# Light experts on their own TensorE arm, and wider rows of expert weights

## The chip, the cores and the metric

The kernel runs on one core of one Trainium2 chip. The metric is device time in microseconds (us) of one execution. Matrix work runs on PE (its weight loads appear as PEld), elementwise work on DVE and ACT, a little on POOL; SP issues the transfers from HBM.

## The reference, cut to what matters

A trunk of two layers: each has a token mixer and a feed-forward part. That of the first layer is dense; that of the second, which the change touches, is a mixture of eight experts with two experts for each of 256 tokens. Everything is float32.

```
D_MODEL, D_FF, N_EXPERTS, TOP_K, SEQ = 1024, 3584, 8, 2, 256
logits = (hf @ router_w) + router_b
top_logit, top_idx = lax.top_k(logits, TOP_K)
top_w = jax.nn.softmax(top_logit, axis=-1)
# for each expert e, on the tokens that chose it:
y = (jax.nn.silu(xb @ w1[e]) * (xb @ w3[e])) @ w2[e]     # xb: rows x 1024
# each token's output is the sum of its two experts' y, weighted with top_w
```

The three matrices of one expert are 1024x3584, 1024x3584 and 3584x1024 floats, 44.04 MB; those of all eight are read once, 352 MB.

## The kernel before, in words

The program is written in phases. The last, `e1`, is the expert stage: from some 985 us to the end. `route` (line 1158) ranks the experts of each token, computes each token's slot within its expert (`pos`) and the weights. `gather` (line 1246) picks, for two experts at a time, the rows by a matmul with one-hot matrices `pe` (slot number equals `pos`), and leaves them transposed and split in two parts, `gh` and `gl`, since the fast matmul type (fp32r) keeps fewer bits than float32. A product of two float32 matrices is then three fast matmuls: high by high, low by high, high by low.

The weights go through the class `Weights` (line 1198). A unit is 1 MiB, loaded by SP into a ring of buffers named `raw` (11 in this phase), cast to `hi` by ACT in two halves (line 1227, ring `hl` of three), and subtracted to `lo` by DVE in one instruction (line 1231, two buffers). An expert has 42 units: seven blocks of 512 hidden columns, each with two units of w1, two of w3 (four times 128 rows of 512 columns, so rows of 2 KB) and two of w2 (rows of 4 KB). Loads, casts and subtractions are issued in the order of the units; `weights.next` keeps one unit ahead of the one that is multiplied.

For each block `hidden` (line 1315) multiplies w1 (`up`, lines 1291, 1292 and 1294: eight matmuls with the high weights, four with the low ones, for each unit), then w3, and forms silu(a) * b, `s1`, on ACT and DVE. `turned` transposes the block before on PE (line 1331) and splits it (lines 1335, 1336). `down` (lines 1349, 1351) multiplies that by w2 into two PSUM banks that collect over the seven blocks. The matmuls are all 128 rows by 512 columns, whether an expert has 40 rows or 128. `finish` scatters an expert's result back with matmuls (lines 1365, 1366), spread over the next expert by `step`; `finish_last` does so at the end (line 1379). If an expert had over 128 rows, a second pass under `tc.If` (line 1464) would run; its code is jumped over.

What sets the order is the program's text and a scheduler that keeps it on each engine apart from a few priorities; each engine runs its own list and waits on semaphores. A `raw` buffer comes free when DVE has subtracted its unit.

## Time and profile before

| | us |
|---|---|
| median of three runs | 2018.96 (2017.47 to 2019.13) |
| the profiled execution | 2017.74 |
| its span in the trace | 2016.0 |
| expert weights' matmuls in it | 1006.26 to 2000.2 |

| engine | busy us | share of the span |
|---|---|---|
| PE | 1926.9 | 96% |
| DVE | 1601.0 | 79% |
| ACT | 1271.1 | 63% |
| POOL | 49.0 | 2% |

The trace is one execution. Durations of PE overlap, since its matmuls are pipelined, so its pace is read from the starts of neighbouring instructions. "Idle before" is how long an engine stood before an instruction, with the operation that released it. PEclk is the granted TensorE clock as a share of the full one: 1.00 is 2.4 GHz and 0.50 is 1.2 GHz.

### The profile page before, as it was taken

How to read it: one execution, taken by the hardware profiler on the slowest of the kernel's cores; microseconds unless marked ns; L12 is line 12 of the kernel's file. 1: busy time of each engine (PE TensorE's matmuls, PEld its weight loads, DVE VectorE, ACT ScalarE, POOL GpSimd, SP SyncE). 2: the span in 40 equal slices, each digit the busy share in tenths (PEclk: the TensorE clock that was granted, in tenths of full speed). 3: DMA queues.
4: the chain of work that ended last, by engine and by line, in shares of the span. 5: the costliest groups of instructions: out<-in, count | busy, mean ns of one | idle time of the engine just before them, and what ended most of it. 6: DMA issues, size and time to landing. Idle time of an engine off the chain costs nothing.

```text
span 2016.0 us, 36973 instructions
## 1 busy us (share of the span) xinstructions
PE 1926.9 (96%) x15372; PEld 1666.4 (83%) x15372; DVE 1601.0 (79%) x1880; ACT 1271.1 (63%) x1810; POOL 49.0 (2%) x55
## 2 busy tenths in 40 slices
PE   5899999999999899999899999999999999999997
PEld 2889889999998798889778788787887878878785
DVE  3778687787666877787588988889898898898887
ACT  2755655544444755655477777677776777777774
POOL 0101000000000101000000000000000000000000
PEclk8999999999999999999899999999999999999999
DMA  8544546698762544456789999999999999999992
GB/s 279 172 155 129 168 146 221 213 311 272 252 215 86 168 153 137 155 169 219 282 311 373 352 335 358 351 371 347 344 356 346 375 352 329 362 345 381 355 363 83
DMA packets 283540, 538.82 MB, mean 267 GB/s; under 512 B 13602, under 2 KB 120548, under 8 KB 283364
## 3 DMA queue, kind: packets, MB, share of 16 engines
q1 hardware_dynamic: 278448, 536.02, 75.6%
q8 instruction: 122, 2.00, 0.4%
q10 hardware_dynamic: 4916, 0.35, 0.2%
q14 instruction: 54, 0.44, 0.1%
HBM read 535.27 MB, written 1.06 MB: 266 GB/s over the span
## 4 chain that ended last, share of the span: by engine, by line
PE 77%; DVE 12%; ACT 5%; DMA 4%; issue 2%; ACTq 0%; DVEq 0%; POOL 0%; POOLq 0%; SPq 0%
PE g L1294 10%; PE a L1349 10%; PE g L1292 9%; PE g L1291 9%; PE g L375 7%; PE g L379 7%; PE g L377 7%; PE a L1351 5%; DVE lo L1231 3%; DMA raw<-in_moe_w_dram 2%; DVE hl L340 2%; DVE t L627 2%; PE a L1055 1%; PE a L1056 1%; PE a L1057 1%
## 5 line engine op out<-in xcount | busy, mean ns | idle before, releaser
L1231 DVE TENSOR_TENSOR lo<-raw,hl 128x2048 fp32r<-128x2048 f32 (+1 forms) x338 | 755.7, 2274 | 45.5 <-ACT hl L1227 40.5
L1227 ACT CAST hl<-raw 128x1024 fp32r<-128x1024 f32 x672 | 653.6, 1049 | 6.3 <-PE g L1292 4.8
L340 DVE TENSOR_TENSOR hl<-raw,hl 128x1024 fp32r<-128x1024 f32 (+1 forms) x252 | 298.3, 1189 | 135.7 <-ACT hl L339 135.1
L339 ACT CAST hl<-raw 128x1024 fp32r<-128x1024 f32 (+1 forms) x252 | 256.8, 1022 | 199.8 <-PE g L379 132.3
L1292 PE MATMUL g<-hl,r 128*128 128x512 f32 x896 | 349.5, 390 | 1.9 <-DVE r L1282 1.9
L1291 PE MATMUL g<-hl,r 128*128 128x512 f32 x896 | 350.6, 391 | 0.1
L1294 PE MATMUL g<-lo,r 128*128 128x512 f32 x896 | 244.7, 395 | 8.5 <-DVE lo L1231 8.5
L375 PE MATMUL g<-r,hl 128*128 128x256 f32 x1536 | 234.4, 292 | 6.6 <-ACT r L483 3.4
L377 PE MATMUL g<-r,hl 128*128 128x256 f32 x1536 | 227.1, 287 | 0.0
L379 PE MATMUL g<-r,hl 128*128 128x256 f32 x1536 | 222.4, 286 | 0.5 <-DVE hl L340 0.5
L375 PEld LDWEIGHTS g<-r,hl 128*128 128x128 f32 x1536 | 203.4, 193 | 15.4 <-ACT r L483 4.7
L1294 PEld LDWEIGHTS g<-lo,r 128*128 128x128 f32 x896 | 163.9, 188 | 51.0 <-DVE lo L1231 19.8
L377 PEld LDWEIGHTS g<-r,hl 128*128 128x128 f32 x1536 | 203.3, 194 | 2.2 <-issue 1.8
L379 PEld LDWEIGHTS g<-r,hl 128*128 128x128 f32 x1536 | 201.2, 193 | 2.7 <-issue 1.9
L1292 PEld LDWEIGHTS g<-hl,r 128*128 128x128 f32 x896 | 168.2, 188 | 38.1 <-DVE r L1282 2.2
L1291 PEld LDWEIGHTS g<-hl,r 128*128 128x128 f32 x896 | 168.2, 188 | 36.5 <-ACT r L1281 0.4
L1351 PE MATMUL a<-hl,t2r 128*128 128x512 f32 x448 | 174.5, 390 | 0.0
L1349 PE MATMUL a<-hl,t2r 128*128 128x512 f32 x448 | 174.2, 389 | 0.0
L1335 ACT CAST t2r<-a 128x512 fp32r<-128x512 f32 x56 | 32.8, 586 | 161.4 <-PE a L1331 161.4
L1349 PE MATMUL a<-lo,t2r 128*128 128x512 f32 x448 | 125.2, 401 | 2.2 <-DVE lo L1231 2.2
L1351 PEld LDWEIGHTS a<-hl,t2r 128*128 128x128 f32 x448 | 84.0, 188 | 18.0 <-DVE t2r L1336 0.4
L1349 PEld LDWEIGHTS a<-hl,t2r 128*128 128x128 f32 x448 | 84.0, 188 | 17.8 <-ACT t2r L1335 0.2
(321 smaller groups left out, 2122.4 us busy)
## 6 DMA issues: line engine op xcount, KB each, us to landing
raw<-in_moe_w_dram SPq DMA_DIRECT2D x334, 1024.0 KB, 7.5
raw<-in_w_in_dram SPq DMA_DIRECT2D x60, 1024.0 KB, 5.4
raw<-in_ffn_w_dram SPq DMA_DIRECT2D x42, 1024.0 KB, 5.8
raw<-in_ada_w_dram SPq DMA_DIRECT2D x40, 1024.0 KB, 5.6
f<-in_ada_w_dram SPq DMA_DIRECT2D x8, 1024.0 KB, 7.8
raw<-in_w_up_dn_dram SPq DMA_DIRECT2D x8, 1024.0 KB, 4.9
raw<-in_w_out_dram SPq DMA_DIRECT2D x8, 1024.0 KB, 4.8
raw<-in_w_up_sb_dram SPq DMA_DIRECT2D x4, 1024.0 KB, 4.9
```

The costliest lines, as they stand in the source:

```text
L339: A.copy(hv, part)
L340: V.tensor_sub(lv, part, hv.bitcast(F32))
L375: T.matmul(pv[:, b, :], hv[:, k, :], xh[:, k, :], start=(k == 0), stop=False)
L377: T.matmul(pv[:, b, :], hv[:, k, :], xl[:, k, :], start=False, stop=False)
L379: T.matmul(pv[:, b, :], lv[:, k, :], xh[:, k, :], start=False, stop=(k == kc - 1))
L1227: self.hi = A.copy(hi[:, h, :], raw[:, h, :])
L1231: V.tensor_sub(lo[:, h, :], raw[:, h, :], hi[:, h, :].bitcast(F32))
L1291: T.matmul(ps, xh[:, 4 * u + k, :], hv[:, k, :], start=(u == 0 and k == 0), stop=False)
L1292: T.matmul(ps, xl[:, 4 * u + k, :], hv[:, k, :], start=False, stop=False)
L1294: T.matmul(ps, xh[:, 4 * u + k, :], lv[:, k, :], start=False, stop=(u == 1 and k == 3))
L1349: T.matmul(ye[nb], gh[:, gs], w[:, k, nw], start=(f == 0 and u == 0 and p == 0), stop=last)
L1351: T.matmul(ye[nb], gl[:, gs], w[:, k, nw], start=False, stop=False)
```

## The change

Each expert's number of rows is counted in `route`, and a flag for each expert (at most 64 rows) is loaded into eight registers of PE (class `Light`). An expert's work now comes in 21 groups of two units. On PE each group is an If with two arms: `heavy`, the three fp32r matmuls as before, and `few`, which reads the unsplit `raw` weights and unsplit rows (`x32`, `g32`) with plain fp32 matmuls on 64 rows; it puts the two halves of the columns on the two halves of the array, output partitions 0 to 63 and 64 to 127. One matmul with `zero` for each product blanks the part of the banks that `few` leaves unwritten. The slots of light experts are moved (`slots`), so that gathered rows stand twice. ACT and DVE cast and subtract each unit in both cases.

Blocks are 1024 hidden columns now (three, and a last one of 512): w1 and w3 come in rows of 4 KB, w2 with two neighbouring rows per partition, 8 KB. `raw` has 7 buffers instead of 11, `hl` 4 instead of 3, `lo` 4 instead of 2. PSUM banks are four for `g` and four for `a`, instead of two and six. The steps of `finish` and `gather` are called in more places.

```diff
     banks_m = dict(g=2, s=2, a=3, v=1)
     phase_f = dict(raw2=3, hl2=3, r8=2, f4=4, t2=4, t2r=4)
-    phase_b = dict(raw2=8, lo=2, r4=6, t2=5, t2r=6, gt=1, xn=2, pe=2, pte=2)
+    phase_b = dict(raw2=4, hl2=1, lo=4, r4=6, x32=3, s32=1, t2=5, t2r=6, gt=1, xn=2, pe=2, pte=2)

     layout_b = dict(
-        t2r=[P, 512], xn=[P, 2, D], pe=[P, 512], r4=[P, KC, P], t2=[P, 512], pte=[P, S], gt=[P, D], raw2=[P, 2048],
-        lo=[P, 2048],
+        t2r=[P, 512], x32=[P, KC, P // 2], s32=[P, 512], xn=[P, 2, D], pe=[P, 512], r4=[P, KC, P], t2=[P, 512], pte=[P, S], gt=[P, D], raw2=[P, 2048],
+        hl2=[P, 2048], lo=[P, 2048],
...
@@ -1171,7 +1171,12 @@
         ps = bank("a")
         T.matmul(ps[:, 0 : 2 * NE], C["before"], oa.rearrange("p b n -> p (b n)"), start=True, stop=False)
         T.matmul(ps[:, NE : 2 * NE], ones, oa[:, 0, :], start=False, stop=True)
+        pc_ = bank("a")
+        for b in range(2):
+            T.matmul(pc_[:, 0:NE], ones, oa[:, b, :], start=(b == 0), stop=(b == 1))
         V.tensor_copy(pos, ps[:, 0 : 2 * NE].rearrange("p (b n) -> p b n", n=NE))
+        V.tensor_copy(rt[:, 5, 0], pc_[:, 0:NE])
+        light = Light(rt[:, 5, 0])
...
+    class Light:
+
+
+        def __init__(self, cnt):
+            self.flag = pc.tile([P, NE], F32, tag="light", name="light")
+            self.int = pc.tile([P, NE], I32, tag="lighti", name="lighti")
+            V.tensor_scalar(self.flag, cnt, float(P // 2) + 0.5, None, ALU.is_lt)
+            V.tensor_copy(self.int, self.flag)
+            self.back = pc.tile([P, NE], F32, tag="back", name="back")
+            V.tensor_scalar(self.back, self.flag, -float(P // 2), None, ALU.mult)
+            self.regs = [
+                nc.values_load(self.int[0:1, e : e + 1], engines=[mybir.EngineType.PE], min_val=0, max_val=1)
+                for e in range(NE)
+            ]
+
+        def slots(self, e):
+
+            t = mk("t2", [P, 512])[:, 0:P]
+            V.tensor_scalar(t, C["iota"], P // 2 - 0.5, self.back[:, e : e + 1], ALU.is_gt, ALU.mult)
+            V.tensor_add(t, t, C["iota"])
+            return t
+
+        def arms(self, e, light, heavy):
+            with tc.If(self.regs[e] > 0) as cmp:
+                light()
+            with cmp.Else():
+                heavy()
...
         def sources(self, j):
             late = None
             for e in range(NE):
-                for f in range(DFF // 512):
-                    w = slice(512 * f, 512 * f + 512)
+                for f, n in self.blocks:
+                    w = slice(f, f + n)
+                    rows = 2048 // n * P
                     for src in (moe_w1, moe_w3):
-                        for u in range(2):
-                            yield src[j, e][512 * u : 512 * u + 512, w], 4, 512
+                        for u in range(D // rows):
+                            yield src[j, e][rows * u : rows * u + rows, w].rearrange("(k p) n -> p k n", p=P), n
                     if late:
                         yield from late
-                    late = [(moe_w2[j, e][512 * f + 256 * u : 512 * f + 256 * u + 256, :], 2, D) for u in range(2)]
+
+                    late = [
+                        (moe_w2[j, e][f + 256 * u : f + 256 * u + 256, :].rearrange("(p k) n -> p k n", k=2), D)
+                        for u in range(n // 256)
+                    ]
...
+        def unit(self, raw, kc, n, parts):
+
             hi = mk(ring("hl"), [P, kc, n], F32R)
             lo = mk("lo", [P, kc, n], F32R)
             for i in range(2):
                 h = slice(i * kc // 2, (i + 1) * kc // 2)
-                self.hi = A.copy(hi[:, h, :], raw[:, h, :])
+                A.copy(hi[:, h, :], raw[:, h, :])
             with tc.issue_after(self.after.ins) if self.after else nullcontext():
                 for i in range(parts):
                     h = slice(i * kc // parts, (i + 1) * kc // parts)
                     V.tensor_sub(lo[:, h, :], raw[:, h, :], hi[:, h, :].bitcast(F32))
-            return hi, lo
...
+            return raw, hi, lo
+
+        def split(self, n):
+            while len(self.ready) < n and self.loaded:
+                self.ready.append(self.unit(*self.loaded.popleft()))
+
+        def group(self):
+
+            self.load(2)
+            self.split(4)
+            return [self.ready.popleft() for _ in range(2)]
...
+            if e0 == 0:
+                weights.after = last
+            x32 = [mk("x32", [P, KC, HS]) for _ in range(2)]
...
+                    G.tensor_copy(x32[e][:, k2, :], t[:, :, 0:HS])
...
+        def up(e, n):
+
+
+
+
+            xh, xl, x32 = gath[e]
+            banks = [bank("g") for _ in range(n // 512)]
+            kc, half = 2048 // n, n // 2
+
...
+            def heavy(u0, units):
+                for u, (_, hv, lv) in enumerate(units):
+                    for w, xs in ((hv, (xh, xl)), (lv, (xh,))):
+                        for k in range(kc):
+                            kk = kc * (u0 + u) + k
+                            for x_ in xs:
+                                for b, ps in enumerate(banks):
+                                    T.matmul(
+                                        ps, x_[:, kk, :], w[:, k, 512 * b : 512 * b + 512],
+                                        start=(kk == 0 and x_ is xh and w is hv), stop=(kk == KC - 1 and w is lv),
+                                    )
+
...
+            def few(u0, units):
+                wide = len(banks) > 1
+                if u0 == 0 and not wide:
+                    blank()
+                for u, (w, _, _) in enumerate(units):
+                    for k in range(kc):
+                        kk = kc * (u0 + u) + k
+                        for i, h in enumerate(halves):
+                            T.matmul(
+                                banks[0][h, 0:half], x32[:, kk, :], w[:, k, half * i : half * i + half],
+                                start=(wide and kk == 0), stop=(kk == KC - 1), skip_group_check=True,
+                            )
+                if u0 == 0 and wide:
+                    blank()
+
+            for u0 in range(0, KC // kc, 2):
+                units = weights.group()
+                light.arms(e, lambda: few(u0, units), lambda: heavy(u0, units))
+                weights.after = None
+                weights.load(5)
+                yield
+            yield banks

...
+        def turned(banks):
+
+            parts = []
...
+                for c in range(4):
+                    at = c // 2 * 256 + c % 2
+                    T.transpose(pg[:, c * P : (c + 1) * P], s1[:, at : at + 255 : 2], ident)
+                gh = mk("t2r", [P, 512], F32R)
+                gl = mk("t2r", [P, 512], F32R)
+                with tc.high_priority(offset=80):
+                    A.copy(gh, pg)
+                    V.tensor_sub(gl, pg, gh.bitcast(F32))
+                    if j == 0:
+                        g32 = mk("s32", [P, 512])
+                        A.copy(g32, pg)
+                parts.append((gh, gl))
+            return parts, g32
...
+            def few(q, units):
+                if first and q == 0:
                     for nb in range(2):
-                        nw = slice(512 * nb, 512 * nb + 512)
-                        last = f == NF - 1 and u == 1 and p == 3
-                        T.matmul(ye[nb], gh[:, gs], w[:, k, nw], start=(f == 0 and u == 0 and p == 0), stop=last)
-                        if p < 2:
-                            T.matmul(ye[nb], gl[:, gs], w[:, k, nw], start=False, stop=False)
+                        T.matmul(ye[nb], zero, parts[0][0], start=True, stop=True, skip_group_check=True)
+                for u, (w, _, _) in enumerate(units):
+                    i, at = (q, u) if n > 512 else (u, 0)
+                    for k in range(2):
+                        gs = slice((2 * at + k) * P + i * HS, (2 * at + k) * P + i * HS + HS)
+                        for nb, h in enumerate(halves):
+                            T.matmul(
+                                ye[nb][h, :], g32[:, gs], w[:, k, 512 * nb : 512 * nb + 512],
+                                start=False, stop=(last and u == 1 and k == 1), skip_group_check=True,
+                            )
+
+            for q in range(n // 512):
+                units = weights.group()
+                light.arms(e, lambda: few(q, units), lambda: heavy(q, units))
+                weights.load(5)
+                yield
...
+        def hidden(e, n, late):
+
+            p1 = up(e, n)
+            next(p1)
+            g = turned(late[3]) if late else None
+            step()
+            for banks in p1:
+                step()
+            ss = [mk("t2", [P, 512]) for _ in banks]
+            for s1, ps in zip(ss, banks):
+                A.activation(s1, ps, AF.Silu)
+            for banks in up(e, n):
+                step()
+            for s1, ps in zip(ss, banks):
+                V.tensor_mul(s1, s1, ps)
+            return ss, g
...
-    with phase("e1", phase_b, dict(g=2, a=6), layout_b):
+    with phase("e1", phase_b, dict(g=4, a=4), layout_b):
```

On PE, at the start of the first expert, the list of before is below: `up` for the second product of the first block, with `r` the gathered rows' parts, `hl` and `lo` a unit's parts, and `g` the PSUM bank.

```order
L1291 MATMUL g_12351<-hl_12333,r_1366_12198 128x512
L1292 MATMUL g_12351<-hl_12333,r_1367_12199 128x512
L1294 MATMUL g_12351<-lo_12334,r_1366_12198 128x512 x4
L1291 MATMUL g_12351<-hl_12354,r_1366_12198 128x512
L1292 MATMUL g_12351<-hl_12354,r_1367_12199 128x512
L1291 MATMUL g_12351<-hl_12354,r_1366_12198 128x512
```

The list of the changed kernel at the same place, the first group of the first expert: `x` is `x32`, and `raw` the unsplit weights.

```order
L1219 COMPARE_AND_BRANCH
L1372 MATMUL g_12394<-raw_1352_12152,x_1375_12307 64x512 x4
L1372 MATMUL g_12394<-raw_1353_12154,x_1375_12307 64x512 x4
L1359 MATMUL g_12395<-r_1377_12309,zero 128x512
L1219 UNCONDITIONAL_BRANCH
L1351 MATMUL g_12394<-hl_1357_12162,r_1377_12309 128x512
L1351 MATMUL g_12395<-hl_1357_12162,r_1377_12309 128x512
L1351 MATMUL g_12394<-hl_1357_12162,r_1378_12310 128x512
L1351 MATMUL g_12395<-hl_1357_12162,r_1378_12310 128x512
```

Each group is now a compare, a light arm of eight 64-row matmuls (and here the blanking one), a jump, and the heavy arm; the heavy arm alternates between two banks.

On SP, in the middle of the stage, before (a row is one load of 1 MiB; in brackets the semaphores that it waits for):

```order
L324 DMA raw_1511_12962<-in_moe_w_dram 128x2x1024 [waits DMAHW0_49,DVE_49]
L324 DMA raw_1514_12981<-in_moe_w_dram 128x4x512 [waits DMAHW1_49,DVE_49]
L324 DMA raw_1518_13001<-in_moe_w_dram 128x4x512 [waits DMAHW2_49,DVE_49]
L324 DMA raw_1521_13020<-in_moe_w_dram 128x4x512 [waits DMAHW3_49,DVE_49]
L324 DMA raw_1525_13040<-in_moe_w_dram 128x4x512 [waits DMAHW4_49,DVE_49]
L324 DMA raw_1532_13070<-in_moe_w_dram 128x2x1024 [waits DMAHW5_49,DVE_49]
```

And in the changed kernel:

```order
L1219 UNCONDITIONAL_BRANCH
L324 DMA raw_1546_13368<-in_moe_w_dram 128x2x1024 [waits DMAHW2_49,DVE_49,PE_49]
L324 DMA raw_1551_13414<-in_moe_w_dram 128x2x1024 [waits DMAHW3_49,DVE_49,PE_49]
L1219 UNCONDITIONAL_BRANCH
L324 DMA raw_1552_13416<-in_moe_w_dram 128x2x1024 [waits DMAHW4_49,DVE_49,PE_49]
L324 DMA raw_1557_13461<-in_moe_w_dram 128x2x1024 [waits DMAHW5_49,DVE_49,PE_49]
L1219 UNCONDITIONAL_BRANCH
L324 DMA raw_13463<-in_moe_w_dram 128x2x1024 [waits DMAHW6_49,DVE_49,PE_49]
L324 DMA raw_13520<-in_moe_w_dram 128x2x1024 [waits DMAHW7_49,DVE_49,PE_49]
L1219 UNCONDITIONAL_BRANCH
```

A load that waited for an earlier transfer and DVE now also waits for PE, and SP has a jump at each group.

On PE, between routing and gather, in the changed kernel (the list of before goes from line 1173 to the gather at once):

```order
L1142 MATMUL s_11803<-t_1331_12096,rw 8x256 x2
L1152 MATMUL a_12126<-cst,t_1338_12124 128x8 x2
L1172 MATMUL a_12184<-rt,cst 128x16
L1173 MATMUL a_12184<-rt,ones 128x8
L1176 MATMUL a_12187<-rt,ones 128x8 x2
L1207 TENSOR_LOAD lighti
L1207 ISA x2
```

Eight such pairs of a load and two register instructions stand there, ahead of the first matmul of the gather.

## Rows read from the trace of the kernel before

**Rows 1.** The page: busy time; weight loads (count, KB, us to landing)
```profile
PE 1926.9 (96%) x15372; PEld 1666.4 (83%) x15372; DVE 1601.0 (79%) x1880; ACT 1271.1 (63%) x1810; POOL 49.0 (2%) x55
...
raw<-in_moe_w_dram SPq DMA_DIRECT2D x334, 1024.0 KB, 7.5
```

**Rows 2.** By stretch: us, busy of each engine, PEclk, DMA share, GB/s
```profile
1450.00:1700.00 250.00, 247.27 (x1129) 202.62 (x1128) 218.75 (x140) 185.67 (x220) 0.00 (x0) 1.00 0.98 354
1700.00:1950.00 250.00, 247.27 (x1117) 202.15 (x1116) 220.77 (x136) 183.99 (x213) 0.00 (x0) 1.00 0.99 359
```

**Rows 3.** Groups by line, 1450 to 1700 us (count, busy, mean ns, idle before)
```profile
L1231 DVE TENSOR_TENSOR lo<-raw,hl 128x2048 fp32r<-128x2048 f32 x85 | 191.2, 2287 | 10.8 <-ACT hl L1227 10.4 <-DMA raw<-in_moe_w_dram 0.4
L1227 ACT CAST hl<-raw 128x1024 fp32r<-128x1024 f32 x170 | 165.4, 1049 | 1.3 <-PE g L1292 1.3
L1291 PE MATMUL g<-hl,r 128*128 128x512 f32 x225 | 88.0, 391 | 0.0
L1292 PE MATMUL g<-hl,r 128*128 128x512 f32 x225 | 87.7, 390 | 0.0
L1294 PE MATMUL g<-lo,r 128*128 128x512 f32 x226 | 61.9, 395 | 2.0 <-DVE lo L1231 2.0
```

**Rows 4.** Waits of SP, 1450 to 1700 us (us in total, times, longest)
```profile
SPq L324 <- DVE lo L1231: 198.2, 80, 6.9
```

**Rows 5.** Waits of PE, 1014 to 1995 us
```profile
PE g L1294 <- DVE lo L1231: 8.5, 17, 1.1
PE a L1349 <- DVE lo L1231: 2.2, 3, 0.7
```

**Rows 6.** Timeline of PE, 1996 to 2005 us (start, us, line, shapes, count)
```profile
1997.31 0.39 PE L1349 MATMUL a<-hl,t2r 128*128 128x512 f32 x1
...
1998.90 0.39 PE L1351 MATMUL a<-hl,t2r 128*128 128x512 f32 x1
...
2000.81 3.70 PE L1379 MATMUL a<-t,pte 128*128 128x512 f32 x8 [0.62 <-DVE t L1374]
```

**Rows 7.** Timeline of PE, start of the expert stage
```profile
999.66 5.85 PE L1266 MATMUL a<-pe,xn 128*128 128x256 f32 x32 [1.82 <-DVE pe L1251]
...
1006.26 0.51 PE L1291 MATMUL g<-hl,r 128*128 128x512 f32 x1
```

**Rows 8.** Timeline of PE, 24 to 37.5 us: matmuls of the conditioning
```profile
24.14 3.56 PE L252 MATMUL g<-f,r 128*32 128x512 f32 x8 [2.21 <-DMA f<-in_ada_w_dram]
...
33.13 1.91 PE L252 MATMUL s<-f,r 128*32 128x512 f32 x8 [0.67 <-DMA f<-in_ada_w_dram]
```

**Rows 9.** Busy time by stretch, four stretches that differ in PEclk
```profile
24.00:27.50 3.50, 3.36 (x8) 0.55 (x8) 3.40 (x19) 0.00 (x0) 0.00 (x0) 0.50 0.95 301
33.00:37.50 4.50, 3.66 (x16) 0.76 (x16) 0.65 (x1) 0.00 (x0) 0.00 (x0) 1.00 1.05 380
650.00:690.00 40.00, 34.83 (x308) 31.04 (x307) 32.85 (x67) 29.71 (x63) 5.39 (x3) 1.00 0.42 138
985.00:1005.00 20.00, 11.89 (x69) 10.00 (x68) 12.31 (x52) 8.80 (x18) 0.00 (x0) 0.74 0.56 208
```

**Rows 10.** Busy time by stretch, two stretches with a full DMA queue
```profile
966.00:981.00 15.00, 15.00 (x114) 13.14 (x114) 7.67 (x13) 7.91 (x15) 0.00 (x0) 1.00 1.05 390
1449.00:1454.00 5.00, 5.00 (x24) 4.16 (x23) 5.00 (x4) 3.33 (x4) 0.00 (x0) 1.00 1.03 413
```

**Rows 11.** Line 1464, the skip of the second pass (ns, start us)
```profile
L1464 POOLq COMPARE_BRANCH  x1: 45/45/45, 1037.7 to 1037.7; - x1
L1464 PEldq COMPARE_BRANCH  x1: 3345/3345/3345, 2002.1 to 2002.1; - x1
```

**Rows 12.** Instructions of line 1532, behind that skip
```profile
L1532 POOLq DRAIN  x3: 34/41/82, 1037.9 to 2015.7; - x3
```

**Rows 13.** Instructions of line 1463, the register load ahead of it
```profile
L1463 SPq TENSOR_LOAD <-mosti x1: 478/478/478, 1969.5 to 1969.5; - x1
...
L1463 SPq SEQ_ASSERT  x1: 33/33/33, 1970.3 to 1970.3; - x1
```

More of the change, by code (lines that the diff above doesn't have):

```diff
@@ L1184, in route @@
         V.tensor_add(wt, wt, tmp)
-        return oa, wt, pos
-    def fullest(oa):
-        ps = bank("a")
-        T.matmul(ps[:, 0:NE], ones, oa[:, 0, :], start=True, stop=False)
-        T.matmul(ps[:, 0:NE], ones, oa[:, 1, :], start=False, stop=True)
-        most = pc.tile([P, 1], F32, tag="most", name="most")
-        mosti = pc.tile([P, 1], I32, tag="mosti", name="mosti")
-        V.tensor_reduce(most, ps[:, 0:NE], AX.X, ALU.max)
-        V.tensor_copy(mosti, most)
-        return mosti
+        return oa, wt, pos, light
+    zero = pc.tile([P, P], F32R, tag="zero", name="zero")
+    most = pc.tile([P, 1], F32, tag="most", name="most")
+    mosti = pc.tile([P, 1], I32, tag="mosti", name="mosti")
+    class Light:
[20 more added lines that the diff above has]
+                heavy()
     class Weights:
+        blocks = [(1024 * i, min(1024, DFF - 1024 * i)) for i in range(-(-DFF // 1024))]
         def __init__(self, j):
             self.coming = self.sources(j)
-            self.ready = deque()
-            self.hi = self.after = None
+            self.loaded, self.ready = deque(), deque()
+            self.after = None
         def sources(self, j):
@@ L1231, in unit, with experts @@
                     V.tensor_sub(lo[:, h, :], raw[:, h, :], hi[:, h, :].bitcast(F32))
-            return hi, lo
-        def fetch(self, n):
-            while len(self.ready) < n and (src := next(self.coming, None)):
-                self.ready.append(self.unit(*src))
-        def next(self):
-            self.fetch(1 + 1)
-            return self.ready.popleft()
-    def experts(l, weights, xnh, xnl, oa, wt, pos, merge):
-        NF = DFF // 512
+            return raw, hi, lo
[6 more added lines that the diff above has]
+            return [self.ready.popleft() for _ in range(2)]
+    def experts(l, weights, xnh, xnl, oa, wt, pos, light, merge):
+        blocks = weights.blocks
         pes = {}
+        HS = P // 2
+        halves = [slice(0, HS), slice(HS, P)]
         def gather(e0):
@@ L1283, in gather @@
             for e in range(2):
-                gath[e0 + e] = parts[e]
-        def up(xh, xl):
-            ps = bank("g")
-            for u in range(2):
-                hv, lv = weights.next()
-                for k in range(4):
-                    T.matmul(ps, xh[:, 4 * u + k, :], hv[:, k, :], start=(u == 0 and k == 0), stop=False)
-                    T.matmul(ps, xl[:, 4 * u + k, :], hv[:, k, :], start=False, stop=False)
-                for k in range(4):
-                    T.matmul(ps, xh[:, 4 * u + k, :], lv[:, k, :], start=False, stop=(u == 1 and k == 3))
-            return ps
+                gath[e0 + e] = *parts[e], x32[e]
@@ L1423, in moe @@
         weights = Weights(j)
+        G.memset(zero.bitcast(F32), 0.0)
         with tc.high_priority(offset=0):
-            weights.fetch(2)
-        oa, wt, pos = route()
+            weights.load(5)
+            weights.split(2)
+        oa, wt, pos, light = route()
         xnh = mk("xn", [P, 2, D], F32R)
@@ L1465, in moe @@
             V.tensor_scalar(pos, pos, float(-P), None, ALU.add)
-            experts(l, Weights(j), xnh, xnl, oa, wt, pos, merge)
+            V.tensor_scalar(rt[:, 5, 0], rt[:, 5, 0], float(-P), None, ALU.add)
+            weights = Weights(j)
+            weights.load(5)
+            weights.split(2)
+            light = Light(rt[:, 5, 0])
+            experts(l, weights, xnh, xnl, oa, wt, pos, light, merge)
     with phase("m0", phase_m, banks_m):
```

105 lines of the change are left out of this document (54 added, 51 removed).

## The prediction

> **What bounds the kernel now.** The page first: PE is busy 96% of the span, and no other engine comes near [rows 1]. Then the expert stage alone, since the change touches nothing else. In a stretch of 250 us there PE is busy 247, DVE 219, ACT 186, and the DMA queue moves 354 GB/s [rows 2]. The groups of that stretch say what fills the engines [rows 3]: DVE subtracts 85 units of 1 MiB at 2.287 us, ACT casts them in two halves of 1.049 us, and PE runs three matmuls for each chunk and unit. The waits of SP show that the loads stand at the buffers: 198 us of waiting for DVE's subtraction of an older unit [rows 4]. So the DMA share near 1 is a queue that is kept full, not a queue that limits. PE itself waited 8.5 and 2.2 us for a `lo` in the whole stage [rows 5]. PE is the bound there, and DVE follows 12% behind it.
>
> How fast PE goes is read from starts, not from durations, since matmuls overlap: seven steps take 1998.90 − 1997.31 = 1.59 us, 0.227 us for each 128x512 matmul [rows 6]. An expert has 42 units and 504 such matmuls: 114.4 us. The stage's weight matmuls run from 1006.26 to 2000.2 us (2000.81 less the idle 0.62) [rows 6, 7], 994 us for eight experts, so 124.2 for one and 248.5 for two. Of the 124.2, 114.4 are weight matmuls, 1.3 the waits for `lo`, and some 8.5 the transposes, gathers and closings.
>
> **Who takes which arm.** The reference's inputs route 77, 41, 65, 56, 80, 43, 90 and 60 rows to experts 0 to 7 (worked out from the reference). Experts 1, 3, 5 and 7 have at most 64: four light experts, in turn with four heavy ones. No expert has over 128, so the second pass is still skipped.
>
> **A light expert on PE.** The three matmuls of 0.227 us per 512 columns and chunk go, and an fp32 matmul on 64 rows comes, for two column halves at once. The trace of before has no 64-row pair, so two rows bound it. A whole-width fp32 matmul shows as two records, one after the other: 8 records in 3.70 us, 0.44 us each [rows 6]. The conditioning matmuls are fp32 too, with 32 output rows in neighbouring column groups: there 8 records take 1.91 us though each lasts 0.59, so (1.91 − 0.59)/3 = 0.44 for each two records, two at a time [rows 8]; the clock was at full there [rows 9]. The change has 84 such couples for each expert. With overlap a couple is 0.88 us: 84 × 0.88 = 73.9 us, and the blanking matmuls (2.3 by ten of 0.227) and the 8.5 of other work bring it to 85. Without overlap it is 168 × 0.88 + 11 = 159. I take 85, since the row nearest in kind (fp32, partial columns, neighbours) shows the overlap; 159 is a rival below.
>
> **What is late next in a light expert.** Not PE. The splits stay: ACT and DVE still split each unit, read or not. DVE needs 219 us for each 250 of the stage [rows 2], so 218 for a pair and 109 for one expert, plus two slot operations of at most 0.7 us; ACT needs 42 × 2 × 1.049 = 88 and four more casts of 0.6. The loads are 44.04 MB for one expert: at 390 GB/s (2 KB rows, queue full) 113 us, at 413 (w2's 4 KB rows) 107, and at the stage's mean of 354, 124 [rows 2, 10]. The rows now come as 4 and 8 KB, so I take 400, about the middle of the two full stretches: 110. DVE and DMA thus both ask for about 110, and a light expert costs 111. Buffers can shift this: PE enters a light expert with up to four split units and more landed ones ahead of it, and may leave it ahead of DVE, since the light arm waits for the load alone. That is at best 105, or less with the debt paid at the start of the next heavy expert; a pair cannot fall below DVE's 218 to 222 or the load's 88.08 MB / 0.400 = 220. I keep 111, since once a block PE's transposes wait for DVE's product of the two hidden banks, and DVE has splits of later groups ahead of it: that keeps PE from leaving DVE far behind.
>
> By the Trainium skill (DMA: Bandwidth & Descriptors, Specifications) HBM gives one core about 358 GB/s; by that a light expert would be 123 us and the whole some 2010. The stretches of 390 and 413 GB/s [rows 10] disagree with it as a limit for this core, and the measurement decides; the rule's result stands below as the weak case.
>
> **A heavy expert.** The same 504 matmuls, in blocks of 1024 columns, with `hl` and `lo` four deep instead of three and two: 114.4 + 8.5 = 123, the `lo` waits gone. New are 21 group boundaries, each a compare and a jump on PE. Branches of before: POOL's jump over about 12 instructions of the built program started at 1037.7 and its next instruction stood at 1037.9; PE's over about 4,500 took 3.345 us [rows 11, 12]. A group's arm is at most some 24 matmuls, so the near row is nearer: 0.2 us, two for a group, 0.4 × 21 = 8 us if bare. I cost them at nothing, because PE's sequencer runs ahead of its array: its branch of 2002.1 was issued while the matmuls of line 1379 ran until 2000.81 + 3.70 = 2004.51, a lead of 2.4 us [rows 6, 11]. Cover gone, 123 becomes 127 to 131. The other engines get 168 jumps each too; on DVE, the second bound, 21 × 0.2 = 4 us for an expert if nothing covers them.
>
> **Buffers and the added wait.** `raw` goes from 11 units to 7, and a load now waits for PE as well as for DVE; behind it on SP stand all later loads, and for those PE and both splitters wait. In a heavy expert up to four of the seven can lie split but unpassed, which leaves three on their way: three units in a landing time of 7.5 us [rows 1] are 420 GB/s, over the 358 that 44.04 MB in 123 us asks for. So I cost it at nothing in a heavy expert; if it binds, loads fall back to the stage's 354, which is the weak case. The gather's POOL copies and the extra `s32` cast run on engines with room [rows 1, 3].
>
> **The start.** PE gets eight register loads between the routing's matmuls and the gather. SP's like load took 0.478 us, and its check stood 0.8 us behind the load's start [rows 13]: 8 × 0.85 = 7 us, and the 1.8 us that PE waits ahead of the gather anyway [rows 7] can cover some. Between 0 and 8, I take +6.
>
> **The sum.** A pair is 123 + 111 = 234 instead of 248.5: −14.5, four times −58. The last expert is light and nothing heavy comes behind it, so its lead of some three units need not be paid back: −8. The start +6. Together −60 against the profiled execution: 2017.74 − 60 = 1957.7. The median stands 1.2 above that execution, so 1959, **1960** rounded.
>
> **The rivals.**
> (a) *Branches are dear.* If a group's two jumps cost as PE's far one, 2 × 3.345 − 2.4 = 4.3 us in each of 84 heavy groups: +361, about 2320, and more with DVE's and ACT's jumps in the light ones. It decides from 0.7 us per heavy group (84 × 0.7 = 59 eats the gain). For it: all long branches of this trace are dear [rows 11]. Against: POOL's near one is not [rows 12]. The Trainium skill (Runtime: NRT & Kernel Launch, Instruction fetch mechanics) says that a taken branch stalls when its target lies outside the window of instructions on hand; POOL's and PE's rows agree with it, and by it most jumps over one arm would be free, those that leave the window not. A middle case, one in five of the 168 jumps of heavy groups dear: 34 × 3.3 = 112 bare, or 34 × 0.9 = 31 behind the lead, so 1990 to 2070.
> (b) *The column halves do not overlap.* Light PE 159: a pair is 123 + 159 = 282, +34, with the start 2017.74 + 134 + 6 = 2158. Against: [rows 8].
> (c) *The clock falls in light experts.* PE would work 85 of 111 us, in bursts of 3.5 us (74 in 21 groups) with about 1.2 us idle between. At low clock the same conditioning matmuls took 3.56 us against 1.91 [rows 8, 9], (3.56 − 1.06)/3 = 0.83 for two records; a light expert would be 84 × 1.66 + 20 = 160, all in all 2160. It decides when more than half of the light work runs low. For it: a stretch in which PE was busy 11.89 of 20 us showed a mean clock of 0.74. Against: one with 34.83 of 40 kept 1.00 [rows 9]; 85 of 111 lies between, nearer to the second.
> (d) *Weak.* Loads keep to 354 to 360, or some branches are bare: light 118 to 124, heavy 123 to 127, 1990 to 2014.
> (e) *No change*: what the light arms give, boundaries take.
>
> **How the numbers follow.** Forecast (1925 to 1990, the low end from pairs at 222 with the last expert's lead) 0.66; weak 0.11; no change 0.04; slower 0.19, of which branches 0.08, clock 0.06, no overlap 0.05. The range **1925 to 2030** leaves out the far parts of the slower cases. A measurement of this kernel tells about 0.2% from no change, so faster 0.77 (forecast and weak), same 0.04, slower 0.19.
>
> **What would show it.** In a heavy expert: starts 0.227 us apart, no idle time of PE at the 21 boundaries, about 123 us from first to last weight matmul. In a light one: two records every 0.44 us, granted clock 1.00, about 111 us, the queue at 390 GB/s or more, PE idle on loads or SP on DVE. The gather at most 8 us later. I am wrong if boundaries show idle time of over 0.7 us (a), if light records come one at a time (b), if the clock row falls in every second eighth of the stage (c), or if light experts stand near 124 us with the queue near 355 GB/s (d).

## The result

| | before | after |
|---|---|---|
| median of the runs, us | 2019.05 (four) | 1971.37 (four, 1966.01 to 1972.13) |
| profiled execution: time, span, us | 2017.74, 2016.0 | 1972.13, 1970.3 |
| mean granted clock of the span | 0.986 | 0.965 |

The changed kernel takes 0.9752 of the time of before, 95% interval 0.9723 to 0.978: 47.7 us less, where 59 were forecast, and inside the range of 1925 to 2030.

The page of the changed kernel answers to [rows 1]: PE is still the busiest engine, but no longer by much, and a unit of weights lands in 7.0 us, before in 7.5.

```profile
PE 1823.6 (93%) x14868; PEld 1412.8 (72%) x14868; DVE 1599.0 (81%) x1900; ACT 1283.3 (65%) x1842; POOL 80.0 (4%) x88
...
raw<-in_moe_w_dram SPq DMA_DIRECT2D x334, 1024.0 KB, 7.0
```

The stretches below are cut at the first weight matmul of an expert: a heavy expert, a light one, and the last light one (columns as in [rows 2]).

```profile
1244.50:1364.80 120.30, 119.87 (x540) 96.07 (x538) 107.73 (x66) 92.24 (x107) 0.00 (x0) 1.00 0.98 369
1364.80:1483.50 118.70, 101.90 (x461) 42.09 (x460) 110.76 (x82) 96.35 (x121) 10.17 (x8) 0.91 0.97 371
1842.70:1950.60 107.90, 92.60 (x423) 36.32 (x422) 106.83 (x66) 91.39 (x106) 0.00 (x0) 0.95 0.97 385
```

In the heavy stretch PE is busy 119.9 of 120.3 us, as it was in the whole stage before. In the light one it is busy 101.9 of 118.7, at a mean clock of 0.91, and DVE, with 110.8, is the busiest engine. The queue moves 371 GB/s there, against 354 in [rows 2]. This pair takes 239.0 us, and the other middle pair, from 1483.52 to 1722.42, takes 238.9; before they took 249.9 and 249.4. (Cut in this way, one group of the heavy expert's second product lies in the light stretch, and one of the light expert's in the next heavy one, so these two numbers mix the arms by some 2 us; their sum does not.)

The beginning and the end of the stage, from PE's timeline:

```profile
998.34 0.61 PE L1172 MATMUL a<-rt,cst 128*128 128x16 f32 x2 [3.65 <-DVE rt L1170]
...
999.22 1.00 PE L1176 MATMUL a<-rt,ones 128*128 128x8 f32 x4
1006.72 5.76 PE L1314 MATMUL a<-pe,xn 128*128 128x256 f32 x32 [6.51 <-issue]
...
1012.86 2.08 PE L1351 MATMUL g<-hl,r 128*128 128x512 f32 x8
```

```profile
1943.74 3.65 PE L1454 MATMUL a<-raw,s 128*64 128x512 f32 x16
1950.64 3.65 PE L1454 MATMUL a<-raw,s 128*64 128x512 f32 x16 [3.25 <-ACT s L1420]
1955.13 3.70 PE L1493 MATMUL a<-t,pte 128*128 128x512 f32 x8 [0.84 <-DVE t L1488]
```

The gather starts 7.1 us later than in [rows 7], behind 6.5 us without a matmul, and the first weight matmul stands at 1012.86 instead of 1006.26. The weights end at 1955.13 − 0.84 = 1954.3 instead of 2000.2. So the start costs 6.6, the stage falls from 993.9 to 941.4 us, and the tail behind it is as long as before. Of the 6.6 us, 1.5 lie ahead of the register loads: the matmuls of line 1172 start at 998.34, and in the trace of before at 996.82.

The light arm's own rows are the couples. Sixteen records take 3.65 us (the row at 1943.74), two at a time: (3.65 − 0.59) / 7 = 0.44 us for each two, which is what the conditioning matmuls showed in [rows 8].

The register loads and the branches of PE (the times in ns are shortest, median, longest):

```profile
L1207 PEldq TENSOR_LOAD <-lighti x8: 297/302/492, 1000.9 to 1005.9; - x8
```

```profile
L1219 PEldq COMPARE_BRANCH  x252: 65/179/413, 1010.9 to 1950.7; - x126
```

The eight register loads start 0.71 us apart (1000.9 to 1005.9). The 252 compares and jumps on PE took at most 0.41 us and 0.18 in the median, where the far one of [rows 11] took 3.3.

The longest waits that answer to [rows 4, 5], over the whole stage (total us, times, longest):

```profile
PE a L1412 <- DVE t L1519: 34.5, 12, 5.0
```

```profile
SPq L324 <- PE g L1351: 268.5, 109, 12.5
SPq L324 <- DVE lo L1271: 231.9, 156, 3.3
SPq L324 <- PE a L1443: 120.2, 28, 5.1
```

PE now waits above all at line 1412, the transposes, for DVE's product of the hidden banks (line 1519). Loads wait for PE more than for DVE.

### The profile page after: what moved, and what is told of

Same layout as the page of the kernel before. It is cut to its first block, busy times and chain, and to the rows that moved or that the text cites. A ratio compares the mean times of both kernels' runs of the same rounds, so it can differ in the third digit from the quotient of the medians.

```text
span 1970.3 us, 36475 instructions
## 1 busy us (share of the span) xinstructions
PE 1823.6 (93%) x14868; PEld 1412.8 (72%) x14868; DVE 1599.0 (81%) x1900; ACT 1283.3 (65%) x1842; POOL 80.0 (4%) x88
## 4 chain that ended last, share of the span: by engine, by line
PE 63%; DVE 18%; ACT 8%; issue 7%; DMA 4%; DVEq 0%; SPq 0%; ACTq 0%
PE g L1351 15%; PE g L379 7%; PE g L375 7%; PE g L377 7%; DVE lo L1271 7%; PE a L1438 4%; PE g L1372 3%; ACT hl L1267 3%; DMA raw<-in_moe_w_dram 2%; PE a L1454 2%; PE a L1443 2%; DVE t L627 2%; DVE hl L340 2%; ACT hl L339 1%; PE a L1055 1%
## 5 line engine op out<-in xcount | busy, mean ns | idle before, releaser
L1351 PE MATMUL g<-hl,r 128*128 128x512 f32 x896 | 222.9, 391 | 0.0
L1372 PE MATMUL g<-raw,x 128*64 128x512 f32 (+1 forms) x1024 | 212.1, 563 | 0.0
L1351 PEld LDWEIGHTS g<-hl,r 128*128 128x128 f32 x896 | 167.4, 188 | 37.0 <-ACT hl L1267 2.4
L1372 PEld LDWEIGHTS g<-raw,x 128*64 128x64 f32 x1024 | 71.5, 141 | 114.6 <-issue 104.2
L1454 PE MATMUL a<-raw,s 128*64 128x512 f32 x448 | 120.2, 684 | 3.6 <-ACT s L1420 3.2
L1351 PE MATMUL g<-lo,r 128*128 128x512 f32 x448 | 120.7, 391 | 0.5
L1351 PEld LDWEIGHTS g<-lo,r 128*128 128x128 f32 x448 | 83.6, 188 | 20.0 <-DVE lo L1271 2.9
L210 DVE SCALAR_TENSOR_TENSOR f<-raw,csil,f 128x1024 f32<-128x1024 f32 x70 | 92.5, 1322 | 5.7 <-DMA raw<-in_ada_w_dram 5.2
L1438 PE MATMUL a<-hl,t2r 128*128 128x512 f32 x224 | 89.0, 397 | 1.7 <-ACT hl L1267 1.7
L1454 PEld LDWEIGHTS a<-raw,s 128*64 128x64 f32 x448 | 34.3, 157 | 74.5 <-issue 67.3
L1443 PE MATMUL a<-hl,t2r 128*128 128x512 f32 x224 | 87.5, 390 | 0.0
```

The source lines that it names most:

```text
L1351: T.matmul(ps, x_[:, kk, :], w[:, k, 512 * b : 512 * b + 512], start=(kk == 0 and x_ is xh and w is hv), stop=(kk == KC - 1 and w is lv),)
L1372: T.matmul(banks[0][h, 0:half], x32[:, kk, :], w[:, k, half * i : half * i + half], start=(wide and kk == 0), stop=(kk == KC - 1), skip_gr ...
L1438: T.matmul(ye[nb], gh[:, gs], w[:, k, nw], start=(first and q == 0 and u == 0 and p == 0), stop=(last and u == 1 and p == 3),)
L1443: T.matmul(ye[nb], gl[:, gs], w[:, k, nw], start=False, stop=False)
L1454: T.matmul(ye[nb][h, :], g32[:, gs], w[:, k, 512 * nb : 512 * nb + 512], start=False, stop=(last and u == 1 and k == 1), skip_group_check= ...
```

## The experiments

All experiments are edits of the changed kernel, so they are compared with its 1971.37 us (ratio 0.9752 to the kernel before). Every ratio below is to the kernel before.

### All experts heavy

```diff
-            V.tensor_scalar(self.flag, cnt, float(P // 2) + 0.5, None, ALU.is_lt)
+            V.tensor_scalar(self.flag, cnt, -0.5, None, ALU.is_lt)
```

> The flag is set to 0 for every expert, so all eight take the heavy arm; blocks, rows, rings, branches and the register loads stay. Theory: branches and the smaller raw ring cost nothing, the waits for lo (10.7 us before) go, the start costs 6.6: 2019 - 10.7 + 6.6 = about 2015, range 2008 to 2017. Rival, boundaries cost a bare 0.2 to 0.4 us per group (168 groups): 2048 to 2082. Rival, the wider rows or the new block order make the heavy arm itself faster (its 120.3 us per expert in the changed kernel): eight times 120.3 from 1012.9 plus 16 = 1991.

Measured: 2015.62 us, ratio 0.9984 (0.9974 to 0.9994). The first weight matmul and the one behind the last:

```profile
1014.16 2.08 PE L1351 MATMUL g<-hl,r 128*128 128x512 f32 x8
```

```profile
2001.96 3.70 PE L1493 MATMUL a<-t,pte 128*128 128x512 f32 x8 [0.62 <-DVE t L1488]
```

From 1014.16 to 2001.96 − 0.62 = 2001.34 are 987.2 us, 123.4 for one heavy expert on the average; it was forecast at 123. The average is of two kinds. Experts 2, 4 and 6, from first weight matmul to first weight matmul, take 121.6 us each; experts 1, 3 and 5, in which the gather for the next two experts runs, take 127.3. The whole run is some 3 us faster than the kernel before, so nearly the whole gain comes from the light arm: the new blocks, rows, rings, branches and register loads together are worth those 3 us.

### All experts light

```diff
+            V.tensor_scalar(self.flag, cnt, 1000.5, None, ALU.is_lt)
```

> The flag is set to 1 for every expert; experts with over 64 rows then lose rows, the work of a light arm is the same. Theory: a light expert is held by DVE's and ACT's splits fed by the loads, 115 to 119 us each without a heavy one to refill buffers: 1012.9 + 8 x 117 + 16 = 1965, range 1945 to 1985. Rival, the light arm is held by PE's own waits and half clock, which a heavy neighbour brings on: then PE's work alone, some 92 us, and DVE's 111 decide: 1915. Rival, a light expert lives on the buffers that the heavy one filled: over 122 each, over 2000.

Measured: 1929.31 us, one run. The edges of the stage, and in it expert 2 and expert 3:

```profile
1012.06 3.65 PE L1372 MATMUL g<-raw,x 128*64 128x512 f32 x16
```

```profile
1912.33 3.70 PE L1493 MATMUL a<-t,pte 128*128 128x512 f32 x8 [0.84 <-DVE t L1488]
```

```profile
1230.58:1340.14 109.56, 93.61 (x424) 35.02 (x421) 105.97 (x66) 90.12 (x106) 0.00 (x0) 0.91 1.01 400
1340.14:1459.23 119.09, 99.78 (x454) 39.58 (x452) 111.86 (x83) 97.35 (x122) 10.18 (x8) 0.90 0.98 375
```

From 1012.06 to 1911.49 are 899.4 us, 112.4 for one light expert on the average. That is under the 115 to 119 that I expected and close to the 111 of the prediction, but it again hides two kinds. Experts 2, 4 and 6 carry no gather and take 109.6 us: DVE is busy 106.0 of them, and the queue is full all the time, at 400 GB/s. Experts 1, 3 and 5, with the gather for the next two, take 119.1: DVE has 5.9 us more to do, it stands still for 7.2 us instead of 3.6, and the queue moves 375 GB/s in the row shown. PE's mean clock is nearly the same in both.

Four heavy experts at 123.4 and four light ones at 112.4 are 943.3 us; the changed kernel's stage took 941.4. That the averages fit so well is partly luck, since in the changed kernel every gather inside the stage falls into a light expert. Taken by kind, experts 0, 2, 4 and 6 of the heavy run (114.4 and three times 121.6) and 1, 3, 5 and 7 of the light run (three times 119.1, and 114.0) make some 950 us, about 10 more than the mix took.

### No branches

```diff
-            with tc.If(self.regs[e] > 0) as cmp:
-                light()
-            with cmp.Else():
-                heavy()
+            if e % 2:
+                light()
+            else:
+                heavy()
```

> The arms are chosen while the program is written (odd experts light, as the routing has it): no compare, no jump, no register load; all else stays. Theory: branches are hidden, so only the 6.5 us of register loads at the start go: 1965, range 1962 to 1967. Rival, the boundaries cost 0.2 us each where an engine is bound: 168 x 0.2 = 34 more, 1931.

Measured: 2008.72 us, ratio 0.995 (0.9933 to 0.9968), 37 us slower than with branches. Neither theory expected that. ACT's and DVE's timelines in a heavy expert show where the time goes:

```profile
1253.41 5.79 ACT L1263 CAST hl<-raw 128x1024 fp32r<-128x1024 f32 x6
1263.45 1.09 ACT L1511 ACTIVATE t<-g 128x512 f32<-128x512 f32 x2 [4.25 <-PE g L1347]
1264.42 11.48 ACT L1263 CAST hl<-raw 128x1024 fp32r<-128x1024 f32 x12
```

```profile
1253.86 8.89 DVE L1267 TENSOR_TENSOR lo<-raw,hl 128x2048 fp32r<-128x2048 f32 x4
1266.45 8.90 DVE L1267 TENSOR_TENSOR lo<-raw,hl 128x2048 fp32r<-128x2048 f32 x4 [3.70 <-ACT hl L1263]
```

ACT stands 4.25 us for PE at the Silu of line 1511, with twelve casts behind it, and DVE 3.7 us for the first of these. Over the stage ACT stands some 70 us for PE at the Silu, 8 in the changed kernel, and DVE waits 102 us for casts, 46 in the changed kernel (the first line is this run's):

```profile
DVE lo L1267 <- ACT hl L1263: 101.6, 71, 4.7
```

```profile
DVE lo L1271 <- ACT hl L1267: 46.4, 47, 2.3
```

Without the Ifs the Silu stands ahead of casts that could have run. That the scheduler was free to place it there, and that an If holds the order of what stands around it, is the likely reason; no run shows it. So this run does not price the branches, and another one was made for that.

### Twice the branches

```diff
-                light.arms(e, lambda: few(u0, units), lambda: heavy(u0, units))
+                for us in (lo_, hi_):
+                    light.arms(e, lambda: few(u0, units, us), lambda: heavy(u0, units, us))
```

`lo_` and `hi_` give the first and the second unit of the group; `down` is changed alike.

> Each group's If becomes two, one for each unit, with the same matmuls: 168 more compares and as many more jumps. Theory: branches hide behind the lead of PE's sequencer, 1971 within 3 us. Rival, a boundary costs a bare 0.2 to 0.4 us where PE is bound (84 more in heavy experts): 1988 to 2005. Rival, the Ifs as fences set the order and more of them change it: a shift either way, with other waits in front of DVE and ACT.

Measured: 1970.44 us, ratio 0.9762 (0.9746 to 0.9779).

```profile
L1219 PEldq COMPARE_BRANCH  x504: 65/176/439, 1009.7 to 1949.6; - x168
```

Twice as many compares and jumps, as long as before, and no change of the time: these near branches cost nothing here.

### Narrow rows

```diff
-            queued(rv[:, k, :], src[:, k, :])
+            for c in range(0, n, wide or n):
+                queued(rv[:, k, c : c + (wide or n)], src[:, k, c : c + (wide or n)])
```

`wide` is 512 for w1 and w3; w2 goes back to `"(k p) n -> p k n"`, and the transposes to columns in a row. A unit of w1 or w3 then comes in two transfers, so that the size of the transfers changes with that of the rows.

> The arms stay, the rows go back: w1 and w3 units are loaded as two column halves (2 KB rows, two transfers), w2 as rows of 4 KB. Theory: in light experts the loads share the bound with the splits, and fall from about 400 to 390 GB/s when full, 3 to 5 us in each of four light experts, nothing in heavy ones: 1983 to 1992. Rival, the loads wait for buffers anyway: 1971. Rival, row size decides (358 GB/s): light experts of 124 us, 1995 or more.

Measured: 1968.74 us, ratio 0.9754 (0.9736 to 0.9772): no difference. A stretch with a full queue, here and in the changed kernel:

```profile
1386.00:1391.00 5.00, 5.00 (x28) 2.37 (x26) 5.00 (x4) 3.85 (x4) 0.00 (x0) 1.00 1.05 388
```

```profile
1386.00:1391.00 5.00, 5.00 (x28) 3.70 (x28) 5.00 (x5) 3.91 (x5) 0.00 (x0) 1.00 1.03 410
```

In this stretch the rate is lower with the narrow rows, 388 against 410 GB/s with the queue full, but the time of the kernel is no longer: the wider rows are a part of the change that brings nothing by itself.

### Light experts without splits, with half the loads, and with neither

The first leaves out the casts and subtractions of experts 1, 3, 5 and 7:

```diff
+            if light:
+                return raw, None, None
```

> Units of experts 1, 3, 5 and 7 are neither cast nor subtracted (their heavy arm, which this routing never takes, holds the light one). Theory: in light experts DVE's 42 subtractions hold the time together with the loads; without them the loads (44.04 MB at 400 to 413 GB/s, 107 to 110 us, less what is landed at the start) decide, light experts fall from 118.7 to 104 to 110: 1971 - 4 x 9 to 15 = 1912 to 1936. Rival, PE's waits for the product and its half clock hold light experts: they stay, 1965 or more. Rival, the loads alone hold them at 371 GB/s: 1965 or more, with DVE idle.

Measured: 1956.93 us, ratio 0.9697 (0.9681 to 0.9714), 14 us less, where 35 or more were expected.

The second loads half of each of their units and reads it twice:

```diff
+            if half and parts == 1:
+                k = slice(0, kc // 2)
             queued(rv[:, k, :], src[:, k, :])
+        if half and parts == 1:
+            return raw[:, :n].unsqueeze(1).broadcast_to([P, kc, n])
```

> Units of experts 1, 3, 5 and 7 are loaded by half; casts, subtractions and matmuls read the loaded half twice, so all other work stays. Theory: in light experts DVE's 110.8 us of work and the loads lie so close that a stall of the one starves the other through the ring of seven; with half the loads the light expert falls to DVE's own time, 111 to 113: 1971 - 4 x 6 = 1947, range 1940 to 1956. Rival, DVE's idle time comes from the order on ACT (casts behind the transposed blocks' casts): light experts stay at 117 to 119, 1966 to 1974. Rival, loads alone hold them: under 110, below 1938.

Measured: 1954.13 us, ratio 0.9672 (0.9656 to 0.9688), 17 us less.

The third does both:

> Units of experts 1, 3, 5 and 7 are loaded by half and neither cast nor subtracted: PE's own work alone is left there. Theory: 84 couples at 0.856 us are 72, with gather, transposes, blanks and closings some 92 us a light expert, heavy ones 123.5 as without the splits: 1957 - 4 x 20 = 1877, range 1865 to 1900. Rival, PE's waits on the transposes' and gather's chain and its half clock hold light experts near 105 or more: 1930 or more.

Measured: 1905.10 us, ratio 0.943 (0.9408 to 0.9452), 66 us less. A light expert in the first, the second and the third, and the heavy one behind it in the third:

```profile
1358.00:1470.00 112.00, 98.85 (x462) 42.22 (x460) 24.11 (x41) 22.68 (x42) 2.14 (x8) 0.94 0.95 369
```

```profile
1359.00:1470.00 111.00, 95.33 (x456) 40.26 (x452) 109.78 (x79) 96.81 (x123) 7.49 (x8) 0.97 0.68 221
```

```profile
1343.00:1450.00 107.00, 99.24 (x485) 45.32 (x484) 27.95 (x44) 27.29 (x48) 2.12 (x8) 0.98 0.67 237
1450.00:1565.00 115.00, 114.03 (x516) 91.90 (x514) 98.73 (x61) 82.43 (x95) 0.00 (x0) 1.00 0.95 356
```

All these light stretches hold the gather for the next two experts. Each resource alone gives little, since another is just behind it. With half the loads the light stretch falls to about 112 us, and DVE fills 109.8 of 111: the light expert at DVE's limit. Without splits it falls to 112 as well, with DVE at 24 us. There the loads and PE are left, and neither is at its limit: the queue moves 369 GB/s, where it moved 400 in the light experts without a gather, and PE is busy 98.9 of 112 us. The heavy expert behind it takes 123.5 instead of 120.3, perhaps because fewer of its units are split ahead; that was not tried. With neither the stretch takes 107, and 222 with the heavy one. That stretch of 107 holds 48 matmuls of the heavy expert's second product (10.9 us) and lacks one group of the light one's (3.65), so the light expert takes 99.8; PE waits 7.7 us in it, and its own work is the 92 of my expectation. The waits are what the expectation left out.

### The rings

```diff
-    phase_b = dict(raw2=4, hl2=1, lo=4,
+    phase_b = dict(raw2=3, hl2=1, lo=4,
```

> The ring of raw units has six buffers instead of seven. Theory: the ring couples loads, splits and PE in light experts, so these grow by 3 to 6 us; heavy ones, where four of the units lie split, grow by up to 3: 1983 to 2005. Rival, seven is more than is used: 1971 within 4.

Measured: 1982.35 us, ratio 0.9817 (0.98 to 0.9833), 11 us more.

```profile
DVE lo L1271 <- ACT hl L1267: 61.7, 65, 3.9
ACT hl L1267 <- DMA raw<-in_moe_w_dram: 61.2, 85, 2.2
```

```diff
-    phase_b = dict(raw2=4, hl2=1, lo=4,
+    phase_b = dict(raw2=5, hl2=1, lo=3,
```

> The ring of raw units has eight buffers, lo three instead of four. Theory: light experts fall by 2 to 4 us, heavy ones gain up to 1 us of waits for lo: 1960 to 1968. Rival, lo's depth carries the step from a light to a heavy expert: heavy ones 3 us longer, 1975 to 1985. Rival, neither matters: 1971 within 3.

Measured: 1968.16 us, ratio 0.974 (0.9724 to 0.9756): not told apart from the changed kernel.

```profile
DVE lo L1271 <- ACT hl L1267: 47.3, 42, 3.9
...
ACT hl L1267 <- DMA raw<-in_moe_w_dram: 1.9, 4, 0.6
```

With six, seven and eight buffers ACT waits 61, 22 and 2 us for loads, and DVE 62, 46 and 47 for ACT. Six buffers are too few. Cut as above, the light stretches, which I expected to grow most, stay at 117.3 to 118.4 us (only the last grows, from 111.6 to 114.4), and the heavy ones take 122.1 to 123.6 instead of 120.3. From seven to eight the loads stop being waited for, and DVE waits for ACT as long as before, though with one buffer of `lo` less.

### The order of the transposes

```diff
             next(p1)
-            g = turned(late[3]) if late else None
+            g = None
             step()
             for banks in p1:
+                if late and not g:
+                    g = turned(late[3])
                 step()
```

> The transposes of the block before stand behind the second group of w1 on PE instead of behind the first, so that DVE's product has 3.5 us more. Theory: PE's 34.5 us of waiting for the product and the half clock behind them go, but DVE and the loads stay the bound: light experts from 118.7 to some 113, as long as all eight light in a row took, since units are freed earlier: 1971 - 4 x 5 = 1951, range 1945 to 1962. Rival, the waits are slack: 1971. Rival, they are the bound: light experts fall by all of 16.8 us of idle time and half clock, to about 100: 1900.

Measured: 1973.12 us, ratio 0.977 (0.9751 to 0.9789): no gain.

```profile
PE a L1412 <- DVE t L1521: 28.8, 9, 4.9
PE a L1314 <- DVE pe L1296: 14.6, 3, 4.9
PE a L1479 <- ACT t2r L1474: 12.7, 8, 2.0
```

PE's waits for the product fell from 34.5 to 28.8 us, and 14.6 us of waits for the one-hot matrices and 12.7 for the closing of an expert came in their place. What PE no longer waited for there, it waited for elsewhere.

### Registers when they are needed

```diff
-            self.regs = [nc.values_load(...) for e in range(NE)]
+        def flagged(self, e):
+            self.regs[e] = nc.values_load(...)
...
             begin(e)
+            light.flagged(e)
```

> Only the first expert's flag is loaded into a register at the start, the others' at the beginning of their expert. Theory: seven of eight loads of 0.8 us go from the start, and the later ones hide behind the sequencer's lead: 1971 - 5.7 = 1966, range 1964 to 1968. Rival, each later load stops PE: 1971.

Measured: 1967.80 us, ratio 0.9752 (0.9736 to 0.9769).

```profile
1000.83 6.13 PE L1316 MATMUL a<-pe,xn 128*128 128x256 f32 x32 [3.11 <-DVE pe L1298]
...
1009.14 1.19 PE L1353 MATMUL g<-hl,r 128*128 128x512 f32 x4 [1.55 <-ACT r L1332]
```

The first weight matmul comes at 1009.14 instead of 1012.86, 3.7 us earlier: the gather then waits for DVE's `pe`, and the first matmul for a cast. The median is lower by as much, but the intervals overlap, so that no run shows it to beat the changed kernel.

## Why the prediction was right, and where it was off

**PE bound in heavy experts, 123 us.** Right on the average of both kinds: 123.4 with all experts heavy. The heavy experts of this routing carry no gather; they take 121.6 in that run, and 120.3 + 1.8 for the cut = 122.1 in the changed kernel.

**PE in a light expert.** The step that the whole forecast hung on, the overlap of the column halves, was right: two records each 0.44 us, as [rows 8] showed, so rival (b) is out. PE's work in a light expert, forecast at 85 us, is 92 by the run without splits and with half the loads. About 3 of the 7 us between are the gather, 5.8 us that fall into the light expert as a whole where the forecast shared them out; the rest was not taken apart. It did not show, since PE was not the bound.

**Light experts bound by DVE and loads, 111 us.** Right in kind, and in size for an expert without a gather: 109.6 where all experts are light. But three of the four light experts of this routing carry a gather. The forecast shared the gather's work out over the pair, 109 us for DVE in each expert, and put nothing for the waits that it brings. In the changed kernel DVE is busy 110.8 us of such a light stretch, and the stretch takes 118.7, or 116.9 with the cut undone; a middle pair takes 239.0 instead of 234. This is the term that was too small. That DVE and the loads both hold the light expert is shown: taking away either gave 14 and 17 us, both 66. Without a gather they run side by side, both nearly full; which of the gather's waits parts them is not shown.

**The last expert, −8.** The size came out, the reason only in part. From first weight matmul to first weight matmul the four pairs took 231.7, 239.0, 238.9 and 231.9 us, and before 244.9, 249.9, 249.4 and 249.7: they gained 13.2, 11.0, 10.5 and 17.8, where 14.5 was forecast for the first three and 22.5 for the last. So the last pair did gain some 7 us more than a middle one. But the last expert also carries no gather, and it holds its own last group on top (3.65 us, and 5.4 in a heavy expert). Before, the two made up for each other. Now, without its last group, the last stretch is 111.6 − 3.65 = 108.0 us, 10.7 under the 118.7 of a middle one. With all experts light, where no heavy expert leaves a lead, the same comparison is 114.0 − 3.65 = 110.3 against 119.1, already 8.8. Some 2 us are left for the lead that the forecast counted; the other 5 of the 7 come from the gather, which is dearer in a light expert, and from the shorter last group, which it did not count. That the term fitted was mostly luck.

**The stage.** It was forecast at 4 × 234 − 8 = 928 us and took 941.4. The some 13 us between lie in all four pairs: 1.3, 3.5, 4.0 and 4.7.

**The start, +6.** Measured +6.6, of which 1.5 lie ahead of the register loads; these stand 0.71 us apart where SP's row gave 0.85.

**Branches, nothing.** Right: no jump over an arm took more than 0.41 us, the 252 of them hide, and 168 more Ifs changed nothing. Rival (a) is out. By the Trainium skill (Runtime: NRT & Kernel Launch, Instruction fetch mechanics) a taken branch stalls when its target lies outside the window of instructions on hand. The rows agree with it so far: the far jump took 3.3 us, and none of the near ones over 0.41.

**The clock, rival (c).** It did fall in light experts, to a mean of 0.91 in their stretches where the forecast had 1.00, behind idle times of 2 to 4 us at the transposes and the gather. It was far from the 160 us of the rival: with all experts light the mean was 0.91 in the experts without a gather too, and these took 109.6 us with DVE busy 106.0 of them. What a faster PE clock alone would bring was not tried.

**The rate of the queue, (d).** The queue gave 410 GB/s when full and 371 on the mean of a light expert, above the 354 to 360 of the weak case, so light experts stayed under its 124 us. The Trainium skill (DMA: Bandwidth & Descriptors, Specifications) has about 358 as a core's limit at the HBM. The 400 GB/s over the whole of expert 2 with all experts light, and the 410 over 5 us, go over it here.

**The buffers.** Costed at nothing in heavy experts, which the 123.4 bears out for seven of them; there was no room to spare, since with six each heavy expert lost 2 to 3 us.

What stays open is why DVE waits for casts in a light expert, 7.3 us of its stretch in the changed kernel. With half the loads it is 0.9:

```profile
DVE lo L1271 <- ACT hl L1267: 7.3, 6, 2.3
```

```profile
DVE lo L1275 <- ACT hl L1271: 0.9, 1, 0.9
```

The order of ACT's work, with casts behind blocks that wait for PE, was the other explanation; with half the loads the program's text for ACT is the same and the waits are nearly gone, so that explanation is not enough by itself. An eighth buffer ended ACT's waits for loads and left DVE's wait in a light stretch nearly as it was, at 6.8. And with all experts light it is 6.9 in an expert with a gather and 3.1 in one without.

## What to carry to other kernels

When a stage's bound is made cheaper, work out every other resource for the same stage: here PE's light arm could have saved 30 us an expert, and DVE and the queue, both some 10% behind, let 11 through on the average, 12 where no gather lay in the expert and 8 where one did. If two resources stand next in line at about the same time, removing one of them is worth little; price the removal of both before building either. And measure an arm by running it alone for all of the work: two such runs gave the size of both terms. But look at its single parts too: work that stands in every second expert, here the gather, may not fall on both arms alike, and an average hides that.

## What was not expected of the hardware

A near compare-and-jump on PE took 0.07 to 0.41 us, and twice as many of them left the time as it was. With the queue full, rows of 4 and 8 KB moved 410 GB/s in a stretch of 5 us, and rows of 2 and 4 KB, in smaller transfers, 388. And a program without the branches was 37 us slower: ACT stood at a Silu with casts behind it.
